# Hybrid decoder layer on one core: half of the in-loop input transposes go to the projection's third PSUM bank instead of attention's transpose bank

## The chip, the cores and the metric

The kernel runs on one core of a Trainium2 chip. The core has five engines with their own in-order instruction streams: TensorE (PE, matmuls and transposes, into PSUM alone), VectorE (DVE), ScalarE (ACT), GpSimd (POOL) and SyncE (SP, which here issues DMAs). They meet through semaphores. PSUM is eight banks of 128 partitions by 512 fp32 numbers. The metric is device microseconds of one execution, median over runs.

## What is computed

One layer of a decoder trunk, 2048 tokens of width 1024, in fp32. A normalised input goes through one projection whose columns feed two groups of heads; their outputs are normalised, joined and projected back; a SwiGLU FFN and a gated embedding follow.

```python
u = rmsnorm(h, attn_pre_norm)
hq, hf, hi, hg, sq, sk, sv = split(u @ w_in)          # 4 x 512 and 3 x 512 columns
o_hg = rmsnorm(hgrn2_mix(hq, hf, hi, lb), hg_out_norm) * silu(hg)   # gated recurrence, 4 heads
o_sb = rmsnorm(stick_breaking_mix(sq, sk, sv), sb_out_norm)         # causal, 8 heads of 64
h = h + rmsnorm(concat(o_hg, o_sb) @ w_out, attn_post_norm)
gate, up = split(rmsnorm(h, ffn_pre_norm) @ w_gate_up)
h = h + rmsnorm((silu(gate) * up) @ w_down, ffn_post_norm)
h = h + (p @ ple_proj) * sigmoid(h @ ple_gate)
```

## The kernel before

**Tiling.** The 2048 tokens are four groups of 512. Every fp32 operand is split into a rounded high part and a low rest (names ending in h and l), and each product is three matmuls, high by high (L224), and the two cross terms (L225, L226). The input of a group must lie with its 1024 features on the partitions: `in_u` makes it in eight steps, one for each 128 features. A step transposes four 128x128 pieces of the normalised tokens (tile `xt`) on PE into one PSUM bank (L316); ACT then writes the high part `uh` out of that bank (L318), and DVE the low part `ul` (L319). Only after L319 may the bank be written again.

**Banks.** The eight banks are handed out by name: three called `mm` for the projections, two called `z` for attention's logits, and one each called `av` (attention's sums), `tr` (attention's transposes) and `hg` (the recurrence). `in_u` gets a list of names and takes them in turn.

**What runs beside what.** The order of PE's instructions is as written; the other engines' orders are set when the program is built, by a scheduler that goes by estimated times. The first two groups are transposed at the start. Then a plan of seven stages runs the projections: the attention columns of groups 1, 2, 3 ("a") and the recurrence columns of groups 0 to 3 ("b"). A projection stage goes in halves of 256 columns. A half holds two of the three `mm` banks and is eight steps of six matmuls each, four steps for each bank, turn about. Between the steps are woven steps of attention and of the recurrence.

**Attention's step.** A unit forms logits (L410, bank `z`), ACT takes two sigmoids (L416, L417), DVE scans them (L431), POOL multiplies (L435, tile `a`). Four units later PE transposes `a` into bank `tr` (L443), ACT and DVE split that into `ah` (L446) and `al` (L448), and one step on PE multiplies `ah` (L459) and `al` (L460) with the values into `av`. There is one bank `tr`, so each L443 needs the L448 before it to be done.

**The tails.** The last three of the 32 slots of stage "b" of group 0 and of group 1 are a tail, in which `in_u` of group 2 or of group 3 is woven in as well: two of its steps ahead of each second step of the projection, six in the tail and the last two directly after it. Of each pair one step goes to bank `hg`, and one, before the change, to bank `tr`. In the first tail ACT also takes the squares (L270) and scales (L307) of the next group's tokens, whose loads from memory (L301) go into tiles that the transposes set free.

**Later.** Attention and the recurrence are followed by the output projections of the groups (`out_proj`, whose weights are split by L210 on ACT and L211 on DVE or POOL), norms of their results (L698 and around it) and the first operand splits of the FFN (L811, L812).

## Time and profile before

| | us |
|---|---|
| median of 3 runs | 3047.1 |
| lowest and highest | 3044.14, 3049.59 |
| profiled execution, its own time | 3042.35 |
| span of the profiled execution | 3040.5 |
| PE busy | 2925.5 (96%) |
| DVE, ACT, POOL busy | 2082.0, 1580.9, 1459.0 |

The profiled execution is one more execution; its span is from the first instruction to the last, and 1.85 us of its time lie around that. "Idle before" a row names the time for which the engine had nothing to do ahead of that row, and who ended it. A row of the waits reads: engine, bank or tile and line that waited, what it waited for, microseconds in total, how often, and the longest.

### The profile page before, as it was taken

Reading aid. Unit: us, or ns where it says so; the run is one execution under the profiler, and the core shown is the slowest. Engines: PE = TensorE matmul, PEld = TensorE weight load, DVE = VectorE, ACT = ScalarE, POOL = GpSimd, SP = SyncE. Lnnn points to the kernel's source line nnn. Section 1 sums busy time; section 2 is a strip of 40 time slices with the busy share of each in tenths; the row PEclk is TensorE's granted clock in tenths of the full one; section 3 lists DMA queues with packets and bytes.
Section 4 is the critical chain, followed back from the end, with each engine's and each line's share of the span. In section 5 each row is a group of like instructions: output and inputs, shape, how many; then the busy total and the mean of one; then the engine's idle time right before and its main releaser. Section 6 shows DMA issues by size and latency. Waiting matters only on the chain.

```text
span 3040.5 us, 52870 instructions
## 1 busy us (share of the span) xinstructions
PE 2925.5 (96%) x18280; PEld 2431.2 (80%) x18280; DVE 2082.0 (68%) x2933; ACT 1580.9 (52%) x3188; POOL 1459.0 (48%) x1410
## 2 busy tenths in 40 slices
PE   8999899999999998898898999999999999999998
PEld 6888788878787787788877878888888888878777
DVE  3556666677677776766697787755887776656775
ACT  5666656666667665667523233454533323545532
POOL 3344445545556665867532232445732321456553
PEclk9999999999999999999999999999999999999999
DMA  7775565455445444457867867667965555677974
GB/s 211 222 212 154 168 181 161 149 158 162 148 130 167 144 132 128 150 192 256 280 205 249 266 218 247 217 201 217 321 214 170 174 173 173 208 218 235 326 241 146
DMA packets 469420, 602.28 MB, mean 198 GB/s; under 512 B 43168, under 2 KB 277664, under 8 KB 469152
## 3 DMA queue, kind: packets, MB, share of 16 engines
q1 hardware_dynamic: 469152, 598.91, 62.7%
q8 instruction: 144, 2.36, 0.3%
q14 instruction: 124, 1.02, 0.1%
HBM read 439.89 MB, written 158.86 MB: 197 GB/s over the span
## 4 chain that ended last, share of the span: by engine, by line
PE 40%; issue 4%; DVE 3%; DMA 3%; POOL 3%; ACT 1%; SPq 0%; POOLq 0%; DVEq 0%; ACTq 0%
PE mm L224 5%; PE mm L225 5%; PE mm L226 5%; PE z L226 4%; PE z L225 4%; PE z L224 4%; PE av L225 2%; PE av L224 2%; PE av L226 2%; PE tr L224 2%; PE tr L226 2%; PE tr L225 2%; POOL wl L812 1%; DVE wl L812 1%; DMA wr<-in_w_gate_up_dram 1%
## 5 line engine op out<-in xcount | busy, mean ns | idle before, releaser
L811 ACT CAST wh<-wr 128x512 fp32r<-128x512 f32 x600 | 351.1, 618 | 473.8 <-PE mm L225 173.5
L812 POOL TENSOR_TENSOR wl<-wr,wh 128x512 fp32r<-128x512 f32 x256 | 371.8, 1459 | 445.2 <-ACT wh L811 413.0
L435 POOL TENSOR_TENSOR a<-be,ring 128x512 f32<-128x512 f32 (+2 forms) x320 | 319.0, 997 | 431.6 <-DVE ring L431 409.6
L224 PE MATMUL mm<-uh,wh 128*128 128x512 f32 x1168 | 485.1, 415 | 3.3 <-DVE eb L336 1.8
L226 PE MATMUL mm<-uh,wl 128*128 128x512 f32 x1168 | 461.4, 395 | 0.0
L225 PE MATMUL mm<-ul,wh 128*128 128x512 f32 x1168 | 459.7, 394 | 1.8 <-POOL ul L812 1.8
L812 DVE TENSOR_TENSOR wl<-wr,wh 128x512 fp32r<-128x512 f32 x344 | 300.3, 881 | 173.2 <-ACT wh L811 157.4
L431 DVE TENSOR_TENSOR_SCAN ring<-z,ring,be 128x512 f32<-128x512 f32 x192 | 245.7, 1280 | 112.3 <-ACT z L417 109.4
L224 PE MATMUL mm<-wh,uh 128*128 128x256 f32 (+1 forms) x992 | 309.8, 312 | 9.8 <-ACT uh L811 9.6
L226 PE MATMUL mm<-wh,ul 128*128 128x256 f32 (+1 forms) x992 | 294.6, 297 | 0.0
L225 PE MATMUL mm<-wl,uh 128*128 128x256 f32 (+1 forms) x992 | 294.3, 297 | 0.0
L226 PEld LDWEIGHTS mm<-uh,wl 128*128 128x128 f32 x1168 | 220.6, 189 | 51.3 <-POOL wl L211 0.3
L224 PEld LDWEIGHTS mm<-uh,wh 128*128 128x128 f32 x1168 | 222.1, 190 | 45.8 <-DVE eb L336 2.2
L225 PEld LDWEIGHTS mm<-ul,wh 128*128 128x128 f32 x1168 | 222.3, 190 | 42.2 <-POOL ul L812 2.2
L448 DVE TENSOR_TENSOR al<-tr,ah 128x512 fp32r<-128x512 f32 (+1 forms) x320 | 192.3, 601 | 92.0 <-ACT ah L446 91.4
L210 ACT CAST wh<-wr 128x512 fp32r<-128x512 f32 x288 | 178.2, 619 | 138.6 <-PE mm L225 85.4
L211 POOL TENSOR_TENSOR wl<-wr,wh 128x512 fp32r<-128x512 f32 x144 | 189.1, 1313 | 108.7 <-ACT wh L210 103.6
L812 POOL TENSOR_TENSOR wl<-s,wh 128x512 fp32r<-128x512 f32 x44 | 100.7, 2293 | 260.8 <-ACT wh L811 206.0
L446 ACT CAST ah<-tr 128x512 fp32r<-128x512 f32 (+1 forms) x320 | 167.5, 524 | 110.6 <-PE tr L443 107.4
L416 ACT ACTIVATE be<-z 128x512 f32<-128x512 f32 (+2 forms) x320 | 171.0, 534 | 87.1 <-PE z L414 37.3
L224 PEld LDWEIGHTS mm<-wh,uh 128*128 128x128 f32 x992 | 192.5, 194 | 18.4 <-ACT uh L811 10.4
L225 PEld LDWEIGHTS mm<-wl,uh 128*128 128x128 f32 x992 | 192.8, 194 | 5.0
(312 smaller groups left out, 7274.0 us busy)
## 6 DMA issues: line engine op xcount, KB each, us to landing
wr<-in_w_gate_up_dram SPq DMA_DIRECT2D x308, 256.0 KB, 3.7
wr<-in_w_in_dram SPq DMA_DIRECT2D x224, 256.0 KB, 3.2
wr<-hid_s SPq DMA_DIRECT2D x154, 256.0 KB, 2.9
wr<-in_w_down_dram SPq DMA_DIRECT2D x110, 256.0 KB, 3.3
hid_s<-hs SPq DMA_DIRECT2D x88, 256.0 KB, 3.5
wr<-wd_s SPq DMA_DIRECT2D x88, 256.0 KB, 3.0
kt<-k_s SPq DMA_DIRECT2D x80, 256.0 KB, 3.0
vt<-v_s SPq DMA_DIRECT2D x80, 256.0 KB, 3.3
```

What stands on the lines that cost most here:

```text
L210: nc.scalar.copy(hi, src)
L211: (lo_engine or nc.gpsimd).tensor_tensor(lo, src, hi.bitcast(F32), op=ALU.subtract)
L224: nc.tensor.matmul(o, l[0], r[0], start=start, stop=False)
L225: nc.tensor.matmul(o, l[0], r[1], start=False, stop=False)
L226: nc.tensor.matmul(o, l[1], r[0], start=False, stop=stop)
L416: nc.scalar.activation(be[:, :n], z[:, :n], AF.Sigmoid, scale=0.125)
L431: nc.vector.tensor_tensor_scan(r[:, o:o + n][:, ::-1], z[:, :n][:, ::-1], be[:, :n][:, ::-1], init, op0=ALU.mult, op1=ALU.bypass)
L435: nc.gpsimd.tensor_tensor(a[:, :n], be[:, :n], r[:, o + 1:o + n + 1], op=ALU.mult)
L446: nc.scalar.copy(hi[:, lo_c:], tr[:, lo_c:])
L448: nc.vector.tensor_tensor(lo[:, lo_c:], tr[:, lo_c:], hi[:, lo_c:].bitcast(F32), op=ALU.subtract)
L811: nc.scalar.copy(hi, src)
L812: lo_engine.tensor_tensor(lo, src, hi.bitcast(F32), op=ALU.subtract)
```

## The change

The second name in the list of banks that `in_u` gets in the two tails is `mm` instead of `tr`. Nothing else is edited.

```diff
         if nxt:
-            un = Stream(in_u(toks, us[nxt], ["hg", "tr"]))
+            un = Stream(in_u(toks, us[nxt], ["hg", "mm"]))
             weave(main, tail, ra.part(tail), (un, 2 * tail, 0))
             main.drain()
             un.drain()
```

In the built program all four `mm` steps of a tail get the same bank, the one of the three that the half in progress does not hold, and the half that comes after the tail gets the two that were held.

PE, first tail, the first pair of `in_u`'s steps (the L224 and L225 rows are the projection's step that follows). The seven other pairs of the two tails differ in the same way:

```order
 L443 MATMUL tr<-ident,a 128x128 x2
 L316 MATMUL hg<-ident,xt 128x128 x4
-L316 MATMUL tr<-ident,xt 128x128 x4
+L316 MATMUL mm<-ident,xt 128x128 x4
 L224 MATMUL mm<-uh,wh 128x512
 L225 MATMUL mm<-ul,wh 128x512
```

On PE the bank's name changes and no instruction changes its place.

ACT, first tail, from the split of the second pair on. Before:

```order
L318 ACTIVATE uh<-hg,g_pre 128x512
L318 ACTIVATE uh<-tr,g_pre 128x512
L416 ACTIVATE be<-z 128x128
L417 ACTIVATE z<-z 128x128
L270 ACTIVATE junk,ss<-xt 128x512
L446 CAST ah<-tr 128x512
L270 ACTIVATE junk,ss<-xt 128x512
L210 CAST wh<-wr 128x512
L416 ACTIVATE be<-z 128x256
```

And with the change:

```order
L318 ACTIVATE uh<-hg,g_pre 128x512
L318 ACTIVATE uh<-mm,g_pre 128x512
L416 ACTIVATE be<-z 128x128
L417 ACTIVATE z<-z 128x128
L446 CAST ah<-tr 128x512
L270 ACTIVATE junk,ss<-xt 128x512
L210 CAST wh<-wr 128x512
L270 ACTIVATE junk,ss<-xt 128x512
L416 ACTIVATE be<-z 128x256
```

Attention's cast L446 now stands ahead of the first square L270, and a weight's cast L210 behind one square instead of two. Further on in this tail the scales L307 move behind the splits L318; DVE's order in both tails stays as it was, but for one row after the first.

POOL, output projection of the third group, the splits of its weights (L211) among splits for the FFN (L812) and sums for the norms (L698, L628). Before:

```order
L211 TENSOR_TENSOR wl<-wr,wh 128x512
L812 TENSOR_TENSOR wl<-wr,wh 128x512
L698 TENSOR_TENSOR h<-h,mix 128x512 x2
L812 TENSOR_TENSOR wl<-wr,wh 128x512
L211 TENSOR_TENSOR wl<-wr,wh 128x512
L272 TENSOR_SCALAR ssum<-ss 128x1
L628 TENSOR_TENSOR oss<-oss,tmp 128x512
```

And with the change:

```order
L812 TENSOR_TENSOR wl<-wr,wh 128x512
L211 TENSOR_TENSOR wl<-wr,wh 128x512
L698 TENSOR_TENSOR h<-h,mix 128x512
L812 TENSOR_TENSOR wl<-wr,wh 128x512
L698 TENSOR_TENSOR h<-h,mix 128x512
L628 TENSOR_TENSOR oss<-oss,tmp 128x512
L211 TENSOR_TENSOR wl<-wr,wh 128x512
```

The first L211 now stands behind one L812, and the second behind one L628 more. Such exchanges of neighbours stand in some twenty places of DVE, ACT, POOL and SP in the output projections and the first FFN block.

## The prediction

> **What bounds the kernel now.** I read the page first, then busy time by stretches, then PE's waits in the stretches that stand out, then the instructions in order of time around those waits.

> ```profile
> span 3040.5 us, 52870 instructions
> PE 2925.5 (96%) x18280; PEld 2431.2 (80%) x18280; DVE 2082.0 (68%) x2933; ACT 1580.9 (52%) x3188; POOL 1459.0 (48%) x1410
> ```

> PE works 96% of the span, the next engine 68%. So time is won only where PE stands still, and the change touches PE in the two tails alone. Busy time by stretches (us, then instructions; after the engines the granted clock, the DMA share and GB/s):

> ```profile
> 110.00:320.00 210.00, 207.29 (x1251) 177.74 (x1250) 124.40 (x182) 130.08 (x280) 90.43 (x96) 0.99 0.64 186
> 320.00:355.00 35.00, 28.18 (x182) 22.44 (x181) 20.72 (x31) 24.77 (x55) 11.76 (x15) 1.00 0.57 181
> 355.00:610.00 255.00, 254.24 (x2251) 214.65 (x2250) 170.97 (x252) 163.80 (x349) 141.23 (x178) 1.00 0.55 162
> 610.00:645.00 35.00, 28.97 (x189) 22.99 (x188) 23.00 (x32) 20.76 (x42) 11.73 (x15) 1.00 0.56 173
> ```

> The tails are the second and the fourth row: PE loses 6.8 and 6.0 us in 35, and next to nothing in the rows around them. No engine in them is full: ACT has 10 us free in the first, DVE 12 in the second. PE's waits there, first tail, then second:

> ```profile
> PE tr L316 <- DVE al L448: 4.4, 3, 1.9
> PE tr L443 <- DVE ul L319: 2.5, 2, 1.6
> ...
> PE tr L443 <- DVE ul L319: 3.2, 3, 1.7
> PE tr L316 <- DVE al L448: 2.8, 3, 2.0
> ```

> All of it is one bank passed to and fro: the input transposes (L316) wait until attention has been read out of `tr` (L448), and attention's transposes (L443) wait until the input has (L319). One case of each on PE, and the read that ends the first:

> ```profile
> 326.19 0.60 PE L316 MATMUL hg<-ident,xt 128*128 128x128 f32 x4
> 328.66 0.66 PE L316 MATMUL tr<-ident,xt 128*128 128x128 f32 x4 [1.87 <-DVE al L448]
> ...
> 345.07 0.66 PE L443 MATMUL tr<-ident,a 128*128 128x128 f32 x4 [1.64 <-DVE ul L319]
> ...
> 351.19 0.66 PE L443 MATMUL tr<-ident,a 128*128 128x128 f32 x4 [0.82 <-DVE ul L319]
> 351.78 0.46 PE L525 MATMUL hg<-q,ks 128*32 128x32 f32 x32
> ```
> ```profile
> 327.01 1.28 DVE L431 TENSOR_TENSOR_SCAN ring<-z,ring,be 128x512 f32<-128x512 f32 x1 [1.96 <-ACT z L417]
> 328.21 0.40 DVE L448 TENSOR_TENSOR al<-tr,ah 128x256 fp32r<-128x256 f32 x1
> ```

> The transposes to `hg` went at 326.19, those to `tr` only at 328.66: the read L448 lies behind a scan of 1.28 us in DVE's order, and the scan waited for ACT.

> **The change part by part.**

> *Removed: the two kinds of wait on `tr`.* 4.4 + 2.5 + 3.2 + 2.8 = 12.9 us, by single rows 6.82 in the first tail and 6.03 in the second. Nothing is added to any engine: the same 16 x 4 transposes, the same splits. If the new bank is free each time and nothing else is late, PE wins 12.9.

> *Added: waits on the third projection bank.* What must have left it are the half before (its last read is L372 below), and then L319 of the `mm` step before:

> ```profile
> 322.50 0.74 DVE L372 SCALAR_TENSOR_TENSOR ev<-mm,g_hg,ev 128x512 f32<-128x512 f32 x1
> 330.08 0.75 DVE L319 SCALAR_TENSOR_TENSOR ul<-tr,g_pre,uh 128x512 fp32r<-128x512 f32 x1 [0.81 <-ACT uh L318]
> 334.51 0.66 PE L316 MATMUL tr<-ident,xt 128*128 128x128 f32 x4 [1.18 <-DVE al L448]
> ```

> The first is done at 323.24, 3 us ahead of need. Of the later ones the row at 330.08 ends at 330.8. Its transposes will run 1.9 earlier and it then follows the `hg` split directly, so it ends near 329.9, while the transposes of 334.51 come to 331.5 (less 1.87 and 1.18). I cost this at nothing; the cover is the 1.6 us from 329.9 to 331.5, which projection and attention fill on PE. Without it each of the six later steps would wait about one ACT and one DVE split, 1.4 us.

> *What is late next, first tail.* ACT is the nearest limit there, since it squares tokens whose loads wait for the transposes:

> ```profile
> 338.95 0.63 ACT L270 ACTIVATE junk<-xt 128x512 bf16<-128x512 f32 x1 [1.62 <-DMA xt<-in_x_dram]
> ...
> 339.58 0.57 ACT L446 CAST ah<-tr 128x512 fp32r<-128x512 f32 x1
> ...
> 346.53 1.34 ACT L307 ACTIVATE xt<-xt,rstd 128x512 f32<-128x512 f32 x2
> ...
> 348.78 0.67 ACT L318 ACTIVATE uh<-hg,g_pre 128x512 fp32r<-128x512 f32 x1
> ```

> From the first square to the split of the seventh step (348.78) ACT takes 9.83 us almost without a pause. In the new order one L446 (0.5) stands ahead of that stretch and two L307 (1.3) behind it: 8.0 us. The loads go out when the fourth step is transposed, 3.05 us earlier (1.87 + 1.18), so the first square stands at 335.9, the split at 343.9, and its low part is done 0.67 + 0.75 later, at 345.3. The recurrence's matmuls, which take bank `hg` after it (the row of 351.78), would be there at 351.78 - 6.82 = 345.0. So 0.3 to 0.5 us come back. Bounds: nothing, and 1.6, if ACT waits for a load once more as at 338.95.

> *What is late next, second tail.* There ACT has no squares. Attention's first transpose of a block needs the product of the unit just before it:

> ```profile
> 614.03 1.28 DVE L431 TENSOR_TENSOR_SCAN ring<-z,ring,be 128x512 f32<-128x512 f32 x1 [1.45 <-ACT z L417]
> 615.39 1.10 POOL L435 TENSOR_TENSOR a<-be,ring 128x512 f32<-128x512 f32 x1 [0.73 <-DVE ring L431]
> 618.07 0.62 PE L443 MATMUL tr<-ident,a 128*128 128x128 f32 x4
> ```

> The last of the four transposes at 618.07 reads this `a`, ready at 616.5. PE gains 1.98 ahead of it and would be there at 616.1 to 616.4: 0.4 comes back (bounds 0 and 1.1, the POOL row). The later steps of this tail keep a microsecond or more.

> Tails: 12.9 - 0.4 - 0.4 = 12.1, and I take off 0.4 for semaphores that now end the wait of something else: **11.7**, between 9.8 (both upper bounds) and 12.9.

> *Moved: neighbours in the output projections.* The quoted place on POOL has prices:

> ```profile
> 1389.29 1.27 POOL L211 TENSOR_TENSOR wl<-wr,wh 128x512 fp32r<-128x512 f32 x1
> 1390.53 1.74 POOL L812 TENSOR_TENSOR wl<-wr,wh 128x512 fp32r<-128x512 f32 x1
> ...
> 1400.32 1.29 POOL L628 TENSOR_TENSOR oss<-oss,tmp 128x512 f32<-128x512 f32 x1 [0.58 <-ACT tmp L627]
> ```
> ```profile
> 1390.61 0.39 PE L225 MATMUL z<-wl,uh 128*128 128x256 f32 x1 [0.96 <-POOL wl L211]
> ...
> 1399.07 0.39 PE L225 MATMUL z<-wl,uh 128*128 128x256 f32 x1 [2.44 <-POOL wl L211]
> ```

> PE already waits for both splits. With L812 ahead of the first it is ready 1.74 later; with L628 ahead of the second, 1.3 later. These don't add: a PE held back at the first arrives later at the second, whose wait of 2.44 takes it up. The net is the later of the two lags, 1.3 to 1.7 us lost. For the other exchanges I know only that their instructions are as long as these (0.2 to 1.8 us) and that half go each way. Value **1.0 lost**, bounds 3 gained and 5 lost.

> Sum: 11.7 - 1.0 = **10.7 us** won. Against the profiled execution 3042.35 - 10.7 = 3031.7. The median of the three runs is 4.75 above that execution, so the time to expect of a median is 3047.1 - 10.7 = **3036.4**.

> **The rivals.**

> *A: the wait moves on to ACT and DVE.* The tails keep half of their waits, as attention's chain of sigmoid, scan, product and cast, and the loads, become what PE waits for: 3047.1 - 6.4 + 1.0 = 3041.7. For it: the scan of 327.01 already waited 1.96 for ACT. Against it: PE gains at most 2 us between two steps, and the rows above leave 0.3 to 3 us of cover at each.

> *B: slower, through the output projections.* The weights' low parts are what PE waits for from 1360 to 1480:

> ```profile
> PE av L225 <- POOL wl L211: 6.5, 4, 3.1
> PE z L225 <- POOL wl L211: 5.7, 4, 2.4
> PE z L225 <- DVE wl L211: 1.7, 1, 1.7
> ```

> If the new orders hold back every one of the nine by a row like that of 1390.53 (1.74) and nothing takes it up, 15.7 us are lost: 3047.1 - 11.7 + 15.7 = 3051. It is slower than before from the seventh on (12.2 us), and by over 0.2% only if the lengthened gaps also cost the clock what C's rows show (6.4): 3057. Against it: only three of the nine stand behind something new in POOL's order, and lags on one queue don't add.

> *C: the clock.* PE's longest gaps among the output projections go with a lower granted clock:

> ```profile
> 1260.50 0.80 PE L460 MATMUL av<-al,vt 128*128 128x512 f32 x1 [3.84 <-DVE al L448]
> ...
> 1283.48 0.46 PE L525 MATMUL hg<-qp,ks 128*32 128x32 f32 x32 [3.26 <-POOL qp L562]
> ```
> ```profile
> 1260.00:1280.00 20.00, 18.51 (x202) 16.48 (x202) 15.76 (x22) 13.26 (x31) 19.47 (x24) 0.83 0.64 201
> 1280.00:1300.00 20.00, 14.84 (x190) 13.34 (x189) 12.44 (x20) 14.80 (x39) 18.34 (x23) 0.85 0.57 187
> ```

> 0.17 and 0.15 of 20 us are 6.4 us lost to it here; the tails, with gaps to 2.0, stand at 1.00. If gaps near 3 us fall otherwise in the changed kernel, this can go, 3036.4 - 6.4 = 3030, or come once more, 3042.8. [...]

> *D: it does not do what it says.* The third bank is not free, and L316 waits on `mm` as it did on `tr`: six later steps by 1.4 leave 12.9 - 8.4 = 4.5, less 1.0: 3043.6. The rows at 322.50 and 330.08 speak against it.

> **How the numbers follow.** My forecast has 0.58; A 0.15; B 0.07; C 0.15, two thirds of it downwards; D 0.05. 0.2% is 6.1 us, about what this measurement tells from no change. Faster by more than that (under 3041.0): the forecast but for 0.03 of it, and C downwards: 0.55 + 0.10, with 0.05 for the milder half of A: 0.70. Slower: B without its mild end, 0.06. The rest, 0.24, is within. The range: below, 3036.4 less C's 6.4 and one more for the run: 3029. Above, to the far side of A and D: 3046. The likeliest case alone, with the bounds of its terms (9.8 - 5 and 12.9 + 3 won), has 3031 to 3042.

> **What will show it.** PE's waits in the two tails: no row of L316 waiting for L448, no L443 for L319, and under 1.5 us of idle time in the two together. A new row of L316 on `mm` is D; new rows of L459, L460, L443 or L525 in the tails above 3 us in all are A. Busy PE in stretches of 35 us from 320 and from about 603 near 34. Between 1360 and 1480 the waits on L211 should stand near 15 us in all, in the place of 13.9; 20 and more is B. The clock by slices from 1240 to 1460 shows C. The prediction is wrong if the tails are clean and the time is not some 10 us less outside C, or if they are not clean.

## The result and the profile after

The changed kernel took 3026.4 us (median of 4 executions, 3025.25 to 3027.35) against 3048.35 of the kernel before beside it (4 executions, 3044.14 to 3049.62). The ratio is 0.9938, 95% interval 0.9922 to 0.9955: 21.9 us, about twice the 10.7 that were forecast, and 2.6 us below the lower end of the range. Over all executions of the study the kernel before has a mean of 3045.5 us (56 executions, standard error 0.6) and the changed one 3025.2 (12, standard error 1.0), a difference of 20.3. The profiled execution of the change took 3025.25 us; its page begins:

```profile
span 3023.1 us, 52860 instructions
PE 2915.8 (96%) x18280; PEld 2424.0 (80%) x18280; DVE 2078.5 (69%) x2933; ACT 1578.7 (52%) x3188; POOL 1450.3 (48%) x1410
```

Already here something shows that the forecast did not have. The span is 17.4 us shorter, and PE's idle time only 7.7 us (span less busy: 115.0 before, 107.3 now). The other 9.7 us are *busy* time of PE, with the same 18280 matmuls. Busy time by stretches in the tails (us, then each engine's busy time and instructions, the granted clock, DMA share, GB/s); the second tail lies some 8 us earlier than before, so its stretch starts at 603:

```profile
320.00:355.00 35.00, 32.36 (x266) 26.27 (x265) 21.81 (x32) 28.72 (x64) 16.45 (x21) 1.00 0.58 179
603.00:638.00 35.00, 34.56 (x280) 27.91 (x278) 28.07 (x37) 24.71 (x50) 15.77 (x19) 1.00 0.62 187
```

PE's idle time was 6.82 and 6.03 in such a stretch; it is 2.64 and 0.44. PE's waits in the two tails (engine, bank and line that waited, for whom, us in total, times, longest):

```profile
PE hg L525 <- DVE ul L319: 1.6, 1, 1.6
PE hg L316 <- DVE ul L319: 1.1, 1, 1.1
...
PE av L460 <- DVE al L448: 0.2, 1, 0.2
PE tr L443 <- POOL a L435: 0.2, 1, 0.2
```

The rows of L316 waiting for L448 and of L443 waiting for L319 are gone, all eleven cases. The first two rows are what is left in the first tail, the last two in the second. In order of time, the first pair of the first tail:

```profile
327.56 0.60 PE L316 MATMUL hg<-ident,xt 128*128 128x128 f32 x4
327.99 0.60 PE L316 MATMUL mm<-ident,xt 128*128 128x128 f32 x4
328.35 0.48 PE L224 MATMUL mm<-uh,wh 128*128 128x512 f32 x1
```

The transposes to `mm` start 0.43 us after those to `hg`. In the rows of before they started 2.47 after them (326.19, 328.66). By the profile, which models the ends of matmuls, the first row ends 0.17 us after the second has begun (328.16 against 327.99); where the next row must wait, its end counts as PE's time.

For the rest of the document the stages are compared with the same matmuls at both ends, since PE's order of work is the same in all these kernels. The table is worked out from the starts of those matmuls and from the clock records of the traces, in which the granted clock is either 1.0 or 0.5 and changes only on a grid of 3.41 us (the profile of before has seventeen stretches at 0.5: twelve of 3.41 us, three of 6.83, one of 13.65, and one that outlasts the span): length in us, in brackets PE's idle time in it, and the number of windows of 3.41 us at half clock. The sum runs from the first matmul to the last, without what lies around them. Means over five profiles with the orders of before, and five with those of the change (four of the changed kernel, and the experiment `hgz`, which has the same orders).

| | first tail (320 to 380) | second tail (600 to 650) | 1100 to 1320 | everything else | sum |
|---|---|---|---|---|---|
| before | 62.7 (8.0; 1.2) | 50.4 (6.0; 0.2) | 217.7 (21.5; 6.4) | 2695.6 (12.2 windows) | 3026.4 (20.0) |
| change | 54.7 (2.5; 0) | 43.5 (0.2; 0) | 213.7 (20.0; 4.8) | 2693.8 (10.4 windows) | 3005.7 (15.2) |
| difference | -8.0 | -6.9 | -4.0 | -1.8 | -20.7 |

The tails give 14.9 us, the output projections' first stretch 4.0, the rest 1.8, almost all of it ahead of 320 us, where the two kernels run the same instructions in the same order.

### The profile page after: what moved, and what is told of

The parts are those of the page before. It is cut to its first block, busy times and chain, and to the rows that moved or that the text cites. A ratio compares the mean times of both kernels' runs of the same rounds, so it can differ in the third digit from the quotient of the medians.

```text
span 3023.1 us, 52860 instructions
## 1 busy us (share of the span) xinstructions
PE 2915.8 (96%) x18280; PEld 2424.0 (80%) x18280; DVE 2078.5 (69%) x2933; ACT 1578.7 (52%) x3188; POOL 1450.3 (48%) x1410
## 4 chain that ended last, share of the span: by engine, by line
PE 44%; POOL 4%; issue 4%; DMA 4%; DVE 3%; ACT 1%; SPq 0%; POOLq 0%; DVEq 0%; ACTq 0%
PE mm L224 6%; PE mm L225 6%; PE mm L226 6%; PE z L226 4%; PE z L224 4%; PE z L225 4%; PE tr L224 2%; PE tr L225 2%; PE tr L226 2%; PE av L226 2%; PE av L224 2%; PE av L225 2%; POOL wl L812 1%; DMA wr<-in_w_gate_up_dram 1%; POOL c L819 1%
## 5 line engine op out<-in xcount | busy, mean ns | idle before, releaser
L812 POOL TENSOR_TENSOR wl<-wr,wh 128x512 fp32r<-128x512 f32 x256 | 374.0, 1468 | 446.9 <-ACT wh L811 423.5
L435 POOL TENSOR_TENSOR a<-be,ring 128x512 f32<-128x512 f32 (+2 forms) x320 | 318.2, 995 | 420.5 <-DVE ring L431 399.2
L224 PE MATMUL mm<-uh,wh 128*128 128x512 f32 x1168 | 483.7, 414 | 3.7 <-DVE eb L336 1.9
L225 PE MATMUL mm<-ul,wh 128*128 128x512 f32 x1168 | 458.3, 392 | 0.1
L812 DVE TENSOR_TENSOR wl<-wr,wh 128x512 fp32r<-128x512 f32 x344 | 299.1, 877 | 176.0 <-ACT wh L811 170.9
L431 DVE TENSOR_TENSOR_SCAN ring<-z,ring,be 128x512 f32<-128x512 f32 x192 | 245.6, 1279 | 108.1 <-ACT z L417 105.1
L224 PE MATMUL mm<-wh,uh 128*128 128x256 f32 (+1 forms) x992 | 307.7, 310 | 9.6 <-ACT uh L811 9.6
L225 PE MATMUL mm<-wl,uh 128*128 128x256 f32 (+1 forms) x992 | 292.5, 295 | 0.0
L224 PEld LDWEIGHTS mm<-uh,wh 128*128 128x128 f32 x1168 | 221.3, 189 | 46.2 <-DVE eb L336 2.3
L225 PEld LDWEIGHTS mm<-ul,wh 128*128 128x128 f32 x1168 | 221.4, 190 | 40.0 <-DVE ul L319 0.5
L448 DVE TENSOR_TENSOR al<-tr,ah 128x512 fp32r<-128x512 f32 (+1 forms) x320 | 191.9, 600 | 84.8 <-ACT ah L446 84.0
L210 ACT CAST wh<-wr 128x512 fp32r<-128x512 f32 x288 | 178.4, 619 | 135.1 <-PE mm L225 79.8
L211 POOL TENSOR_TENSOR wl<-wr,wh 128x512 fp32r<-128x512 f32 x144 | 189.3, 1315 | 108.3 <-ACT wh L210 102.8
L812 POOL TENSOR_TENSOR wl<-s,wh 128x512 fp32r<-128x512 f32 x44 | 103.8, 2366 | 265.5 <-ACT wh L811 201.4
L446 ACT CAST ah<-tr 128x512 fp32r<-128x512 f32 (+1 forms) x320 | 167.5, 523 | 106.9 <-PE tr L443 103.2
L224 PEld LDWEIGHTS mm<-wh,uh 128*128 128x128 f32 x992 | 190.5, 192 | 18.1 <-ACT uh L811 10.4
L225 PEld LDWEIGHTS mm<-wl,uh 128*128 128x128 f32 x992 | 190.8, 192 | 5.0
```

Of the source, the lines that this page charges most:

```text
L210: nc.scalar.copy(hi, src)
L211: (lo_engine or nc.gpsimd).tensor_tensor(lo, src, hi.bitcast(F32), op=ALU.subtract)
L224: nc.tensor.matmul(o, l[0], r[0], start=start, stop=False)
L225: nc.tensor.matmul(o, l[0], r[1], start=False, stop=False)
L431: nc.vector.tensor_tensor_scan(r[:, o:o + n][:, ::-1], z[:, :n][:, ::-1], be[:, :n][:, ::-1], init, op0=ALU.mult, op1=ALU.bypass)
L435: nc.gpsimd.tensor_tensor(a[:, :n], be[:, :n], r[:, o + 1:o + n + 1], op=ALU.mult)
```

## The experiments

**The change as it is, and each tail alone.** The kernel builds both tails with one list of banks; the two experiments give the new bank to one tail and leave the other with `tr`.

```diff
-            un = Stream(in_u(toks, us[nxt], ["hg", "mm"]))
+            un = Stream(in_u(toks, us[nxt], ["hg", "mm" if nxt == 2 else "tr"]))   # first_only
+            un = Stream(in_u(toks, us[nxt], ["hg", "mm" if nxt == 3 else "tr"]))   # second_only
```

> The changed kernel once more, beside the kernel before. Theory T (three parts): in the tails PE's waits fall by about 12 us; the other 5 us between the two profiled executions are the clock, which halved for 22 windows of 3.41 us before and for 16 after (1.7 us each, about 10 us), less about 5 us of longer waits elsewhere. Put over all positions of the windows against the gaps, the gaps of the two traces should give 14.8 and 14.0 half windows, so on average the clock is worth only 1 to 2 us. T then expects the time to spread with the granted clock and a difference of 12 to 17 us between the medians of more runs. Rival S (the tails carry it all, their gaps halve the clock in most executions): 20 to 23 us again, and the kernel before at a mean clock about 0.003 lower. Rival O (the moved neighbours in the output projections carry the rest): 20 to 23 us again with clocks that do not differ.

> The bank is changed in the first tail alone (group 2); the second has attention's bank as before. From the pair of profiles, by the starts of the same PE instructions: the first tail gained 5.1 us, the second 6.6. T: 5 to 7 us below the kernel before, about 3042; the waits of L316 and L443 on each other gone in the first tail and 6 us in the second. S: 9 to 11 us below, about 3038. O: its orders in the output projections are those of neither kernel, so anything from 3036 to 3046 by that part.

> The bank is changed in the second tail alone (group 3). Its orders on POOL and SP stay near those of the kernel before (32 and 49 lines of difference, against 173 and 88 for the whole change). T: 6.6 us and up to 1 of clock below the kernel before, about 3041. S: 10 to 12 below, about 3037. O: only the tail's 6.6, about 3041.5, and first_only and second_only together fall short of the whole change by the 8 us or so that hang on the orders. If the two differences add to that of the whole change, O falls.

Measured: the change again 3024.7 us beside 3044.5 of before, ratio 0.9934 (0.9921 to 0.9947). The first tail alone 3036.5, ratio 0.997 (0.9959 to 0.9981). The second tail alone 3035.9, ratio 0.997 (0.9958 to 0.9982). By the means, 9.5 and 9.1 us under before, together 18.6 of the whole 20.3. Theory T was too low three times: 12 to 17 us for the whole change (19.9 by the medians), 5 to 7 for the first tail, and up to 7.6 for the second. S named the sizes better, if a little high (20 to 23, 9 to 11 and 10 to 12), but its ground, that the tails carry all of it, does not hold (the table has 14.9 of 20.7 there). PE's waits with the first tail alone changed, in its second tail, and then with the second alone, in its first:

```profile
PE tr L443 <- DVE ul L319: 3.3, 3, 1.7
PE tr L316 <- DVE al L448: 2.5, 2, 2.0
```
```profile
PE tr L316 <- DVE al L448: 4.2, 3, 1.9
PE tr L443 <- DVE ul L319: 2.6, 1, 2.6
```

The tail that keeps `tr` keeps its waits, the other is clean: 54.2 us for the first tail in the one kernel, 43.5 for the second in the other, as with the full change. Each of the two kernels has its own orders downstream, and the two gains still add up to the whole within their errors. So most of the gain comes with the tails, and theory O, by which the two would fall some 8 us short of the whole, falls.

But each tail gives some 9 us, and the idle time that went is under 7 in each. Where the rest comes from is seen in the tail that was left as it was. The kernel with the second tail alone, stretches of one window of 3.41 us each in its first tail, and the transposes in the third of them:

```profile
338.40:341.81 3.41, 2.26 (x17) 1.82 (x16) 0.69 (x1) 2.41 (x7) 0.40 (x3) 1.00 0.75 253
341.81:345.22 3.41, 1.25 (x6) 0.68 (x4) 1.84 (x3) 3.41 (x9) 2.39 (x3) 1.00 0.14 21
345.22:348.63 3.41, 3.00 (x9) 2.57 (x10) 1.79 (x3) 3.09 (x7) 0.86 (x2) 0.50 0.32 116
348.63:352.04 3.41, 3.41 (x21) 2.66 (x19) 2.48 (x4) 3.03 (x6) 0.00 (x0) 1.00 0.42 139
```
```profile
345.63 1.12 PE L443 MATMUL tr<-ident,a 128*128 128x128 f32 x4 [2.57 <-DVE ul L319]
```

In the second stretch PE was idle for 2.16 us of 3.41; the third runs at a clock of 0.50, and the transposes of 345.63 take 1.12 us where 0.66 and 0.62 stood for such rows. In the fourth the clock is back. A wait of 2.57 us, shorter than any that I had held against the clock, cost, by estimate, up to 1.7 us more (half of 3.41, at the clock of 0.50).

**Another free bank.** The list is `["hg", "z"]`, one of the two banks of attention's logits. The orders of DVE, ACT, POOL and SyncE are the same as with the change but for the bank's name.

```diff
-            un = Stream(in_u(toks, us[nxt], ["hg", "mm"]))
+            un = Stream(in_u(toks, us[nxt], ["hg", "z"]))
```

> The second name in both tails is attention's logit bank (two banks called z) instead of the third projection bank. All other instructions of DVE, ACT, POOL and SP stand exactly as in the changed kernel. If what counts is only that the input transposes leave the bank of attention's transposes, this is as fast as the changed kernel (within 3 us) and the tails are as clean. If the logits need both z banks there, PE waits on L410 or L316 for the scan L431, up to 1.3 us at each of eight places: up to 10 us slower than the changed kernel, and the difference lies in the tails alone. O: apart from such waits it has the whole gain of the changed kernel, since it has its orders.

Measured: 3027.3 us, ratio 0.9937 (0.9926 to 0.9949), level with the change; tails of 54.7 and 43.5 us, and no logits row (L410) waits in them. What counts is that the bank is free, not that it belongs to the projection.

**No second bank.** Both steps of a pair go to bank `hg`, so `tr` is left alone, and the second step waits for the splits of the first.

```diff
-            un = Stream(in_u(toks, us[nxt], ["hg", "mm"]))
+            un = Stream(in_u(toks, us[nxt], ["hg", "hg"]))
```

> Both steps of each pair go to the recurrence's bank, so that attention's bank is free as in the changed kernel, but the second step of a pair must wait for the two splits of the first (0.68 on ACT, 0.75 on DVE, and the ways between): 1.6 to 2.0 us at each of eight places, 13 to 16 us in the two tails. T: gaps of that size halve the clock in some of the windows, two to four in the tails, 3 to 7 us more; in all 16 to 23 above the changed kernel, near the kernel before (3041 to 3049). If the gaps cost only their own length, 3039 to 3042. O (the place of the gain is the orders on POOL and the rest, which are near those of the changed kernel: 42 and 46 lines of difference on POOL and SP): well below the kernel before, 3030 to 3036.

Measured: 3052.9 us beside 3042.3, ratio 1.003 (1.0016 to 1.0044). PE's waits in the first and in the second tail:

```profile
PE hg L316 <- DVE ul L319: 10.8, 4, 4.3
...
PE hg L316 <- DVE ul L319: 10.8, 4, 3.3
```

That is what the prediction's rival D would have looked like, had the bank not been free. Leaving `tr` alone is not enough; the transposes must also find a bank whose last reader is done. The tails are 66.2 and 59.0 us, 12.1 longer than before by the table, with 7.6 us more of idle time and five windows at half clock instead of 1.4. The waits are 21.6 us, where 13 to 16 were expected, and the time lies above the 3041 to 3049 that theory T had. Theory O (3030 to 3036, since the orders on POOL and SP are near those of the changed kernel) falls a second time. The kernel's mean (3053.2) is 7.7 above that of before, this one profile only 3.2: outside the tails it has 15 windows at half clock, where before has 18.6 on average.

**Before, three more profiles.** The forecast rested on one profile of before; here are others, with nothing edited.

> The kernel before, unchanged, for a second profile. The medians differ by 20 us and the two first profiles by 17, of which the same PE instructions place 12 in the tails, so some 8 us of the median's difference have no place yet. T (tails and chance of the clock): over several profiles the tails of the kernel before cost more than in the first one, because now and then a gap of 1.6 to 2.0 us there halves the clock for a window (1.7 us) as one profile of second_only and one of first_only showed; a mean of 61 to 62 us for the first tail (59.96 in the first profile, 54.8 with the change) and of 50 to 52 for the second (50.12, 43.5). The half windows outside the tails scatter, 12 to 20, as in the changed kernel. S (everything lies in the tails): 64 and 54 on the mean.

> The same once more. T: as for before_a; between the profiles of this kernel the time scatters by 5 to 10 us, and follows the number of half windows at 1.7 us each. If something outside the tails is longer by 2 us and more in each profile of the kernel before than in each of the changed one, that part is the moved neighbours (O) and not chance.

> The same once more, so that four profiles of the kernel before stand against three with the orders of the changed one (the first, again, hgz). T: outside the tails the means of the two differ by under 3 us once half windows are counted off at 1.7 us each. O: by 5 to 8.

Measured: 3044.3, 3038.0 and 3054.1 us. The first tail is 63.6, 62.4 and 67.4 us, where the profile of the forecast has 60.0, and its half-clock windows are 2, 0 and 4, where that profile has none. The second tail is 50.1, 51.7 and 50.1. The slowest one's busy time in its first tail, which begins 1.5 us later there:

```profile
321.50:356.50 35.00, 28.04 (x171) 22.92 (x170) 20.33 (x30) 24.11 (x52) 10.86 (x13) 0.90 0.51 159
```

PE counts as busy for 28.04 us, as in the forecast's row (28.18 at a clock of 1.00), but gets 171 matmuls done instead of 182: the granted clock is 0.90, and what that loses lies inside the busy time.

What differs ahead of the clock are the loads. In the profile of the forecast ACT waited 1.62 us for them before the splits of the third pair, and attention's transposes behind these splits waited 1.64. The same place in the profile of 3044.3 us:

```profile
336.40 0.63 ACT L270 ACTIVATE junk<-xt 128x512 bf16<-128x512 f32 x1 [0.64 <-DMA xt<-in_x_dram]
338.90 0.63 ACT L270 ACTIVATE junk<-xt 128x512 bf16<-128x512 f32 x1 [1.30 <-DMA xt<-in_x_dram]
```
```profile
343.92 1.11 PE L443 MATMUL tr<-ident,a 128*128 128x128 f32 x4 [3.04 <-DVE ul L319]
```

In the three profiles, in their order, ACT waits 1.94, 2.01 and 2.38 us there, and this L443 3.04, 2.25 and 3.44. After the waits of 3.04 and 3.44 the clock is halved, after that of 2.25 it is not. So the first tail's idle time, not only its clock, differs from run to run, and the profile on which I worked was a mild one.

As for the theories, the first tail has a mean of 62.7 us over five profiles and the second 50.4, where T had 61 to 62 and 50 to 52, S 64 and 54. Outside the tails the two orders differ by 5.8 us, and by 3.4 half-clock windows; at 1.7 us each (half of 3.41, an upper estimate) these are 5.8 as well, as T said (under 3 left) and O did not (5 to 8).

**A bank without the last two waits.** The change leaves 2.7 us of waits in the first tail, both on bank `hg`. Here the pair uses a logits bank and the projection's bank, and `hg` stays with the recurrence.

```diff
-            un = Stream(in_u(toks, us[nxt], ["hg", "mm"]))
+            un = Stream(in_u(toks, us[nxt], ["z", "mm"]))
```

> The other bank of each pair is a logits bank (z) instead of the recurrence's bank (hg); the third projection bank stays as in the change. What the change left in the first tail are two waits on bank hg: the recurrence's matmul L525 for the split L319 (1.56 us) and an input transpose for it (1.08 us). Theory H (they come from the shared bank): both rows go, PE is busy 34 to 35 of 35 us from 320, the first tail is 2 to 2.6 us shorter than with the change, and the kernel is 0 to 3 us faster than it (about 3023 us where before is 3045, ratio 0.992 to 0.994). Theory L (they come from ACT, whose squares wait twice for loads): the row of L525 goes, but a row of the same step's split reappears on L224 or on the next L316, the tail stays within 0.6 us of 54.7 us, and the kernel is level with the change (ratio 0.9935). Theory Z: attention's logits, which take the two z banks in turn, wait for the splits instead (rows of L410 waiting for L319 in the two tails, over 3 us), and the kernel is slower than the change by that and by half-clock windows, 3028 us and more.

Measured: 3026.0 us beside 3045.1, ratio 0.9932 (0.991 to 0.9954). PE's waits in the first tail, and the stretch:

```profile
PE mm L316 <- DVE ul L319: 0.6, 1, 0.6
PE mm L224 <- DVE ev L372: 0.5, 1, 0.5
PE z L316 <- DVE ring L431: 0.4, 1, 0.4
PE av L460 <- DVE al L448: 0.2, 1, 0.2
```
```profile
320.00:355.00 35.00, 33.23 (x269) 26.62 (x267) 23.08 (x34) 28.74 (x64) 15.43 (x19) 1.00 0.60 187
```

Both rows on `hg` are gone, as theory H said, and four smaller ones of 1.7 us in all stand in their place; the tail is 54.2 us, 0.5 shorter than with the change, not 2 to 2.6. Theory L named the size and the time rightly (within 0.6 us of 54.7, level with the change), and one of its rows, the next L316 waiting for a split. Theory Z falls: no logits row (L410) waits. In this profile too ACT waits 2.7 us for loads. PE has 1.8 us of idle time left in this tail, each time for a read by DVE, so that another choice of bank has little left to win; no choice of bank that was run beats the change by more than can be measured.

**Chance or order, 1100 to 1320 us.** By then the stretch had 6.75 half-clock windows on average with the orders of before and 4.0 with those of the change. Three more profiles of unchanged code:

> The changed kernel as it is, one more profile for the count of half-clock windows between 1100 and 1320 us, where the change has so far shown 4, 3 and 5 of them and the kernel before 8, 7, 5 and 7. Theory N (chance: by the idle times of PE and a grid of windows whose phase differs from run to run the two orders should have 4.1 and 4.8): this and the next profile of the change together have 4 or more each on average, the further one of the kernel before 5 or fewer. Theory O (the new orders have fewer by themselves): this one 3 to 5, the kernel before 6 to 8. Either way 43.5 us in the second tail, 54.7 in the first, 3025 us.

> The kernel before as it is, a fifth profile. Theory N: 3 to 5 half-clock windows between 1100 and 1320 us and that stretch near 215 us. Theory O: 6 to 8 of them and 217 to 219 us. Tails 60 to 64 and 50.1 to 51.7 us, 3045 us.

> The changed kernel as it is, once more, as a fourth execution with these orders. Theory N: 4 to 5 half-clock windows between 1100 and 1320 us. Theory O: 3 to 5. The two are told apart by the mean of all profiles of each kernel: N expects the difference of the means, now 6.75 against 4.0, to shrink towards 0.7, O expects it to stay above 2. Tails 54.7 and 43.5 us, 3025 us.

Measured: 7 windows (216.2 us), 5 (215.8) and 5 (213.3); 3023.3, 3042.8 and 3021.9 us. The 7 of the changed kernel and the 5 of the kernel before are both outside what theory O had for them and within theory N. The difference of the means has shrunk from 2.75 to 1.6 (6.4 of five profiles against 4.8 of five, `hgz` among them). With a standard error near 0.9 that does not exclude the 0.7 that N expects, nor the 2 and more of O, nor quite exclude none at all. What is not the clock is steadier: PE's idle time in that stretch is 21.1 to 21.9 in the five profiles of before, and 19.0 to 21.1 in the five with the new orders. The matmul whose wait differs most, first before, then with the change:

```profile
1296.13 0.33 PE L460 MATMUL av<-al,vt 128*128 128x128 f32 x1 [1.67 <-DVE al L448]
```
```profile
1280.15 0.28 PE L460 MATMUL av<-al,vt 128*128 128x128 f32 x1
```

It waits 1.65 to 1.73 us in the five profiles of before, and in those with the new orders not at all or up to 0.54: there this split (L448) comes sooner. Another L460 goes the other way, from no wait to 0.85 to 0.99 in four of the five. The balance over all matmuls of the stretch, about 1.5 us of its 4.0, is the orders' own.

## Why the prediction was right, and what was mis-sized

The mechanism, the place and the sign were right; the size was half of what was measured.

**The two kinds of wait on `tr`: right.** Forecast 11.7 net in the tails. PE's idle time there fell by 5.5 and 5.8, 11.3 us, over five profiles each. The pieces differ from the forecast's. Before, an average first tail has 8.0 us of idle time, not the 7.0 of the profile that I had. And more comes back there than "0.3 to 0.5 us": 2.5 remain. The change's first tail, ACT's loads and the two waits on PE:

```profile
332.88 0.63 ACT L270 ACTIVATE junk<-xt 128x512 bf16<-128x512 f32 x1 [1.34 <-DMA xt<-in_x_dram]
335.48 0.63 ACT L270 ACTIVATE junk<-xt 128x512 bf16<-128x512 f32 x1 [1.37 <-DMA xt<-in_x_dram]
```
```profile
338.23 0.66 PE L316 MATMUL hg<-ident,xt 128*128 128x128 f32 x4 [1.08 <-DVE ul L319]
344.00 0.46 PE L525 MATMUL hg<-q,ks 128*32 128x32 f32 x32 [1.56 <-DVE ul L319]
```

The forecast named this wait of L525, at 0.4 us, and for its upper bound the cause, a load that ACT waits for; the wait of 1.08 on `hg` at 338.23 it had not seen. ACT waited twice, 1.34 and 1.37, together 2.71, and PE's two waits are 2.64 together. In the five other profiles where the first tail has a new bank beside `hg`, PE's idle time there is likewise within 0.1 us of what ACT waits for loads (2.0 to 2.5 us): ACT's waits pass to PE almost whole. That the 1.56 is the forecast's upper bound ("1.6, if ACT waits for a load once more") is luck: this wait is 1.56 to 1.57 in all six, and the other one, 0.42 to 1.08, is what follows the loads. The two together are above the bound.

The forecast's own sign, "under 1.5 us of idle time in the two together", was missed: it is 2.7 us by the table. Rival A's sign (rows of L459, L460, L443 or L525 above 3 us in all) was not reached: they are 2.0. The second tail came out as forecast: `a` from L435 is what it waits for, 0.2 us.

**The third bank is free: right.** No row of L316 on `mm` waits for L319. The cover of 1.6 us that I costed at nothing held, and `hghg` shows the price of a bank that is not free.

**The cost of a wait: the first term that was missing.** I had costed each wait at its idle time. PE's busy time in each tail fell by about 0.8 us beside it, without any work less. It sits at the two sides of the waits. From the last transpose to `hg` to the first to `tr` (328.66 in the prediction's rows) 2.14 us pass between the starts, of which 1.87 count as idle: the last matmul ahead of the wait is given 272 ns, where 109 lie between two starts in a stream. The first one after the wait takes 0.06 us more. So a wait cost about 0.22 us above its idle time here. Eleven waits are 2.4; with the four that the change has in the tails, 1.5 us were won. The 163 ns more ahead of a wait rest on the profile's modelled ends, and what fills them no run shows; that they are lost the starts show.

**The clock in the tails: the second.** "The tails, with gaps to 2.0, stand at 1.00" was true of one execution. Over five profiles of before the tails have 1.4 half-clock windows, after the change none: about 2.1 us, what is left of 14.9 after 11.3 of idle time and 1.5 at the sides of the waits. Rival C had the clock, but I looked for it only at gaps of 3 us, and only among the output projections.

**The output projections: wrong sign, within the bounds.** Forecast 1.0 lost, between 3 gained and 5 lost. PE's idle time from 1100 to 1320 fell by 1.5; behind 1320 it differs by less than its scatter. The waits for the weights' low parts, of which rival B feared 15.7 us, between 1340 and 1480 after the change:

```profile
PE z L225 <- POOL wl L211: 6.6, 4, 2.6
PE av L225 <- POOL wl L211: 4.9, 4, 1.5
PE z L225 <- DVE wl L211: 1.7, 1, 1.7
```

13.2 in all, where 13.9 stood and near 15 was forecast. The step that failed is the pricing of two quoted exchanges as if they stood for all of them.

**The rest.** 10.7 forecast; with the terms as measured, 14.9 in the tails and 1.5 from the order, 16.4. The profiles show 20.7. The remaining 4.3 go with half-clock windows outside the tails, 15.2 instead of 18.6: 1.2 of them ahead of 320 us, where no instruction differs and which I therefore put down to chance, 1.6 between 1100 and 1320. Of the latter, theory N's estimate from PE's idle times puts 0.7 (1.2 us) down to the shorter waits of the new orders. That all executions together show 20.3 with a standard error of 1.2 says that some 2.7 us between 17.6 and 20.3 stay unexplained, or are two standard errors of chance. It stays open.

## What to carry to other kernels

Two writers that handed one PSUM bank to and fro on an engine that is otherwise full cost more here than the idle time in the row of waits: 11.3 us of idle time were worth 14.9, with about 0.22 us more at the sides of each wait (1.5 in all) and 2.1 that go with half-clock windows, which followed idle times of 1.98 and 2.16 us in a window (`first_only`, `second_only`) as well as those near 3. Before a fine forecast take more than one profile of the kernel before, above all of a stage with waits of that length, or with waits that hang on loads. And when a transpose gets a new bank, look first at who read the bank last, since either bank that was free did as well here (`mm` 3026.4 us, `z` 3027.3), and the one that was not (`hg`, 3052.9) was slower than before.

## What was not expected of the hardware

The clock. For each of the 14 profiles of this study (five of before, four of the changed kernel, and those of `first_only`, `second_only`, `hgz`, `hghg` and `zmm`) I took from its trace every window of 3.41 us at full clock after the first 30 us, PE's idle time in it, and whether the next window stood at 0.5 in the trace's record of the granted clock.

| PE idle in a window of 3.41 us | windows | next one at half clock |
|---|---|---|
| under 0.5 us | 11261 | 2 |
| 0.5 to 1.0 | 349 | 6 |
| 1.0 to 1.5 | 209 | 13 |
| 1.5 to 1.8 | 67 | 13 |
| 1.8 to 2.2 | 54 | 47 |
| 2.2 to 3.0 | 49 | 49 |
| over 3.0 | 46 | 46 |

```profile
615.55 0.66 PE L316 MATMUL tr<-ident,xt 128*128 128x128 f32 x4 [1.98 <-DVE al L448]
```
```profile
616.14 0.92 PE L316 MATMUL tr<-ident,xt 128*128 128x128 f32 x4 [1.98 <-DVE al L448]
```

The gap is 1.98 us in all five profiles of before. In four the grid cuts it (in one of them 0.1 us from its start) and the tail is 50.1 us long; in this one it lies within a window, the next window runs at half clock, and the tail is 51.7. The number of such windows is part of the scatter of the times, but not all of it: 16 in the profile of 3038.0 us and 23 in that of 3054.1, but 22, 20 and 19 in those of 3042.4, 3042.8 and 3044.3.
